# Mix stage of a decoder layer: the four gate units of the input projection moved to the end of the unit order

## The chip, the cores and the metric

The kernel runs on one core of one Trainium2 chip. A time is the device time of the whole program in microseconds (us). The engines are PE (TensorE, the matrix engine), DVE (VectorE), ACT (ScalarE), POOL (GpSimd) and SP (SyncE, which issues DMAs). Each runs its own list of instructions in a fixed order.

## The reference

One decoder layer over 512 prompt tokens and 8 sequences of 4 new tokens, in float32:

```python
x <- LN1(alpha*x + 0.5*SwiGLU_1(x))
x <- LN2(alpha*x + W_out[concat(attn_group(x), hgrn_group(x))])
x <- LN3(alpha*x + 0.5*SwiGLU_2(x))

z = x @ w_in
qa, ka, va, qh, fh, ih, gh = jnp.split(z, IN_SPLITS, axis=-1)
...
logf = jnp.log(lbh + (1.0 - lbh) * jax.nn.sigmoid(zf))
kh = (1.0 - lbh) * jax.nn.sigmoid(-zf)
qh = jax.nn.silu(qh)
```

The attention group has 8 heads of 64, with rotary positions and a dilated sliding window over keys, in the prompt and against cached keys and values for the new tokens. The other group has 4 HGRN2 heads: a gated recurrence S_t = diag(f_t) S_{t-1} + (1-f_t) outer i_t, with output o_t = S_t^T q_t, a root-mean-square norm per head, and a gate: the output is multiplied by silu(gh). The gate enters only there, at the very end of a head.

## The kernel before

The 544 columns (16 new tokens, 512 of the prompt, 16 new tokens) lie in two halves `a` of 272. Each float32 product is made of three matmuls, xH*wH, xL*wH and xH*wL, where H is the part rounded to the fast matmul format and L what is left (ACT makes H at L332, DVE makes L at L334). The mix stage, between the first FFN and the output projection, has 28 units of the input projection. A unit is 128 output columns: 2 halves x 8 blocks of the contraction x 3 = 48 matmuls (L315, L316, L317). The table `WIN` sets their order: an entry (c, i) is head group c (0 to 3) and kind i: 0 q, 1 k, 2 v, 3 forget gate f, 4 HGRN q, 5 HGRN value, 6 output gate. The weights lie in memory in this order and are fetched ahead through a ring of four. `rounds` runs the first four units side by side, and then one at a time.

What follows a unit hangs on its kind (`mixed`). After v, when q and k are there, comes `att_prompt(c)`: eight steps, four blocks of 128 queries (128, 256, 384 and 512 keys) times two heads. A step is: two score matmuls (L702) into a buffer `ps_a`; mask and negative maximum on DVE (L706, with a readout); exponential on ACT (L708); reciprocal and multiplication on DVE (L709, L710); one to four transpositions on PE (L679); a copy on ACT (L717). After each block of queries come the products with v (L726). Buffers `ps_a` and `aw` are two and three deep. `att_sample`, after head groups 1 and 3, handles the new tokens; it multiplies with cached values in tiles `kv`, fetched three deep by SP from `in_cv` (L784, L790).

After the HGRN value unit comes `hgrn(c)`, with two scans over the columns on DVE (L822, L825), and at its end a function `end`: mean of squares by matmuls (L954), a reciprocal root from logarithm and exponential (table load L435, L443, L446, L453 to L455), products with it, and `update`, which forms the new states (vm at L813, L973, L976). A gate unit makes tanh and a copy of its columns on ACT (L550, L551), their product on DVE (L552), and `gate` multiplies the head's output by it (L964). Two lines choose the order of the two: in `mixed`

```python
                        if WIN[j + 1] != (c, 6):
                            part["end"] = part["end"]()
```

runs `end` at once, without the gate, if the next unit is not the head's own gate, and leaves `gate` for later. Otherwise `end(gs)` runs with the gate unit, and applies the gate first and the norm after it. The order is fixed when the kernel is built: a scheduler simulates the engines over the program as it is written, and lays down a list for each engine. After the mix stage `project` splits the eight head outputs (L332, L334 to xH, xL) and multiplies by w_out; its first units are begun in the tail of the mix stage as their inputs come.

Of the kernel before, what the change touches and what calls it, by code (L numbers as in the profile page):

```python
# [64 lines left out]
def free(t, offset, dims):  # L65
# [3 lines left out]


WIN = (
    (0, 0), (0, 4), (0, 3), (0, 5), (0, 6), (0, 1), (1, 3), (0, 2), (1, 4), (1, 0), (1, 1), (1, 5), (1, 2), (2, 3),
    (2, 0), (2, 4), (2, 1), (2, 2), (1, 6), (2, 5), (2, 6), (3, 0), (3, 1), (3, 2), (3, 4), (3, 3), (3, 5), (3, 6),
)


# [1139 lines left out]
```

## Time and profile before

| | us |
|---|---|
| median of three runs | 1137.05 |
| lowest and highest | 1135.55, 1137.87 |
| profiled execution | 1141.93 |
| span of its instructions | 1140.1 |

The profiled execution had a mean granted clock of 0.982 of TensorE's full speed. A profile line that begins with two numbers and a bar at the end of its name (`| 6.2, 435 |`) gives busy time in us and the mean of one instruction in ns; a timeline row gives start and length in us, and in brackets what it waited for; a window row gives the stretch, its length, busy time and instructions of PE, weight loads, DVE, ACT and POOL, then the granted clock, the share of the DMA engines and GB/s.

### The profile page before, as it was taken

Reading aid. Unit: us, or ns where it says so; the run is one execution under the profiler, and the core shown is the slowest. Engines: PE = TensorE matmul, PEld = TensorE weight load, DVE = VectorE, ACT = ScalarE, POOL = GpSimd, SP = SyncE. Lnnn points to the kernel's source line nnn. Section 1 sums busy time; section 2 is a strip of 40 time slices with the busy share of each in tenths; the row PEclk is TensorE's granted clock in tenths of the full one; section 3 lists DMA queues with packets and bytes.
Section 4 is the critical chain, followed back from the end, with each engine's and each line's share of the span. In section 5 each row is a group of like instructions: output and inputs, shape, how many; then the busy total and the mean of one; then the engine's idle time right before and its main releaser. Section 6 shows DMA issues by size and latency. Waiting matters only on the chain.

```text
span 1140.1 us, 21927 instructions
## 1 busy us (share of the span) xinstructions
PE 1094.2 (96%) x8666; PEld 1047.1 (92%) x8666; DVE 780.7 (68%) x1282; ACT 570.6 (50%) x1123; POOL 373.8 (33%) x420
## 2 busy tenths in 40 slices
PE   7899999999999999999999988988999999999995
PEld 7899999999999988878997858978999999999995
DVE  6868857865776965664746646788687578567766
ACT  5435533552554675566456643465355235425544
POOL 2513412430343444231411301345143125214336
PEclk9899999999999999999999978999999999999998
DMA  7344444454415385376736624504533432332122
GB/s 247 104 130 154 154 144 148 126 194 149 128 44 195 112 276 168 122 261 228 238 105 223 240 98 161 184 17 171 171 130 102 136 111 89 89 103 92 41 72 79
DMA packets 46168, 163.49 MB, mean 143 GB/s; under 512 B 6512, under 2 KB 10224, under 8 KB 45040
## 3 DMA queue, kind: packets, MB, share of 16 engines
q1 hardware_dynamic: 46064, 162.08, 43.0%
q8 instruction: 68, 1.11, 0.4%
q14 instruction: 36, 0.29, 0.1%
HBM read 150.79 MB, written 42.60 MB: 170 GB/s over the span
## 4 chain that ended last, share of the span: by engine, by line
PE 82%; DVE 7%; DMA 4%; ACT 3%; issue 2%; POOL 2%; SPq 0%; POOLq 0%; DVEq 0%; ACTq 0%
PE ps_d L278 20%; PE ps_h L278 10%; PE ps_d L316 7%; PE ps_d L315 7%; PE ps_d L317 7%; PE ps_a L278 5%; PE ps_a L316 3%; PE ps_a L315 3%; PE ps_a L317 3%; PE ps_h L317 2%; PE ps_h L315 2%; PE ps_h L316 2%; DVE wL L334 2%; PE ps_s L754 1%; PE ps_a L679 1%
## 5 line engine op out<-in xcount | busy, mean ns | idle before, releaser
L334 DVE TENSOR_TENSOR wL<-ws,wH 128x1024 fp32r<-128x1024 f32 (+3 forms) x141 | 174.2, 1236 | 80.8 <-ACT wH L332 77.7
L332 ACT ACTIVATE wH<-ws 128x1024 fp32r<-128x1024 f32 (+3 forms) x141 | 129.3, 918 | 183.4 <-PE ps_d L278 49.3
L1008 POOL TENSOR_TENSOR h<-hx,h 128x272 fp32r<-128x272 f32 x88 | 98.6, 1122 | 159.7 <-ACT h L1007 153.4
L334 DVE TENSOR_TENSOR wL<-sw,wH 128x1024 fp32r<-128x1024 f32 x78 | 117.1, 1503 | 40.2 <-ACT wH L332 40.1
L315 PE MATMUL ps_d<-xH,wH 128*128 128x272 f32 x456 | 136.2, 299 | 4.7 <-ACT xH L332 4.3
L316 PE MATMUL ps_d<-xL,wH 128*128 128x272 f32 x456 | 137.4, 301 | 3.2 <-DVE xL L405 3.0
L317 PE MATMUL ps_d<-xH,wL 128*128 128x272 f32 x456 | 135.2, 297 | 0.5 <-DVE wL L334 0.5
L332 ACT ACTIVATE wH<-sw 128x1024 fp32r<-128x1024 f32 x78 | 82.6, 1059 | 81.8 <-PE ps_d L278 29.5
L225 POOL TENSOR_TENSOR sw<-ws,sw 128x512 f32<-128x512 f32 x38 | 55.3, 1456 | 157.3 <-DVE sw L222 137.5
L315 PEld LDWEIGHTS ps_d<-xH,wH 128*128 128x128 f32 x456 | 87.4, 192 | 9.2 <-ACT xH L332 5.0
L278 PE MATMUL ps_d<-xH,wL 128*128 128x272 f32 x320 | 92.9, 290 | 1.9 <-DVE wL L334 1.9
L316 PEld LDWEIGHTS ps_d<-xL,wH 128*128 128x128 f32 x456 | 87.6, 192 | 7.5 <-DVE xL L405 3.7
L278 PE MATMUL ps_d<-tH,wH 128*128 128x272 f32 x320 | 92.9, 290 | 0.0
L278 PE MATMUL ps_d<-tH,wL 128*128 128x272 f32 x320 | 92.9, 290 | 0.0
L278 PE MATMUL ps_d<-tL,wH 128*128 128x272 f32 x320 | 92.9, 290 | 0.0
L220 POOL TENSOR_TENSOR sw<-ws 128x512 f32<-128x512 f32 x38 | 53.2, 1401 | 120.7 <-issue 48.1
L278 PE MATMUL ps_d<-xL,wH 128*128 128x272 f32 x320 | 92.4, 289 | 0.0
L278 PE MATMUL ps_d<-xH,wH 128*128 128x272 f32 x320 | 92.2, 288 | 0.0
L317 PEld LDWEIGHTS ps_d<-xH,wL 128*128 128x128 f32 x456 | 87.6, 192 | 4.1 <-issue 2.7
L315 PE MATMUL ps_d<-h,wH 128*128 128x272 f32 x240 | 69.2, 288 | 0.0
L317 PE MATMUL ps_d<-h,wL 128*128 128x272 f32 x240 | 69.0, 288 | 0.0
L316 PE MATMUL ps_d<-h,wH 128*128 128x272 f32 x240 | 68.9, 287 | 0.0
(412 smaller groups left out, 3600.8 us busy)
## 6 DMA issues: line engine op xcount, KB each, us to landing
ws<-in_w2gu SPq DMA_DIRECT2D x42, 512.0 KB, 3.9
ws<-in_w1gu SPq DMA_DIRECT2D x41, 512.0 KB, 4.5
ws<-in_win SPq DMA_DIRECT2D x28, 512.0 KB, 4.2
out_ck_out<-in_ck SPq DMA_DIRECT2D x16, 640.0 KB, 5.7
out_cv_out<-in_cv SPq DMA_DIRECT2D x16, 640.0 KB, 5.5
kv<-in_ck SPq DMA_DIRECT2D x16, 640.0 KB, 6.3
kv<-in_cv SPq DMA_DIRECT2D x16, 640.0 KB, 5.0
ws<-in_w1d SPq DMA_DIRECT2D x24, 384.0 KB, 3.2
```

The costliest lines, as they stand in the source:

```text
L220: g.tensor_tensor(s2[:, lo], a21, a22, op=OP.add)
L225: g.tensor_tensor(s2[:, hi], a12, s1[:, hi], op=OP.subtract)
L278: nc.tensor.matmul(ps, w[:, k, :], y, start=first and i == 0, stop=last and i == 2, skip_group_check=True)
L315: mm(o, H[:, k, :], x[0], start=first, stop=False)
L316: mm(o, H[:, k, :], x[1], start=False, stop=False)
L317: mm(o, L[:, k, :], x[0], start=False, stop=last)
L332: a = self.nc.scalar.activation(H, x, AF.Copy)
L334: v = self.nc.vector.tensor_tensor(L, x, H.bitcast(F32), op=OP.subtract)
L679: self.nc.tensor.transpose(out, x, self.ident[:n, :n])
L754: last = mm(ps[w, :384], self.qsz[:, i, s, 32 * (b + x):32 * (b + x) + 32], kc[x][:, i, 2 * s:2 * s + 3].rearrange("p s d -> p (s d)"), st ...
L1008: nc.gpsimd.tensor_tensor(L, x, H.bitcast(F32), op=OP.subtract)
```

## The change

Only the table changes. Three gate units, (0,6), (1,6) and (2,6), move from places 5, 19 and 21 to the end, ahead of (3,6), which was last already. By the two lines above, heads 0, 2 and 3 now run `end` without their gate, as head 1 did, and all four multiply by the gate after the norm.

```diff
 WIN = (
-    (0, 0), (0, 4), (0, 3), (0, 5), (0, 6), (0, 1), (1, 3), (0, 2), (1, 4), (1, 0), (1, 1), (1, 5), (1, 2), (2, 3),
...
+    (2, 4), (2, 1), (2, 2), (2, 5), (3, 0), (3, 1), (3, 2), (3, 4), (3, 3), (3, 5), (0, 6), (1, 6), (2, 6), (3, 6),
 )
```

On PE, at the end of the stage: the sixth to eighth steps of the last attention. The names are those of the program, `aw` the probabilities, `ps_a` the scores or their transpositions, and 315 to 317 projection matmuls. Before, from the scores of the sixth step on:

```order
L702 MATMUL ps_a_7647<-klo_4814,qst_7416 128x384
L927 MATMUL ps_h_8165<-ivs_8142,ats_4818 32x256 x4
L930 MATMUL ps_h_8165<-st_8047,smp_8163 32x256 x4
L315 MATMUL ps_d_8349<-xH0_8291,wH_7861 128x272
...
L679 MATMUL ps_a_7655<-mats_69,aw_7650 128x128 x3
L702 MATMUL ps_a_7667<-kst_7498,qst_7416 128x512
L702 MATMUL ps_a_7667<-klo_4814,qst_7416 128x512
L954 MATMUL ps_h_8252<-E2_8051,mats_69 128x272
...
L679 MATMUL ps_a_7675<-mats_69,aw_7670 128x128 x4
```

In the new order, from the last matmul of the output projection's second block on:

```order
L317 MATMUL ps_d_8427<-xH0_8291,wL_8156 128x272
L679 MATMUL ps_a_7441<-mats_69,aw_7436 128x128 x3
L702 MATMUL ps_a_7447<-kst_7299,qst_7216 128x384
L702 MATMUL ps_a_7447<-klo_4814,qst_7216 128x384
L679 MATMUL ps_a_7455<-mats_69,aw_7450 128x128 x3
L702 MATMUL ps_a_7467<-kst_7299,qst_7216 128x512
L702 MATMUL ps_a_7467<-klo_4814,qst_7216 128x512
L973 MATMUL ps_h_8004<-vm_8005,ks3_7944 128x512
...
L679 MATMUL ps_a_7475<-mats_69,aw_7470 128x128 x4
L702 MATMUL ps_a_7482<-kst_7299,qst_7216 128x512
L702 MATMUL ps_a_7482<-klo_4814,qst_7216 128x512
L679 MATMUL ps_a_7490<-mats_69,aw_7485 128x128 x4
```

The norm's mean matmuls (L954) and the new tokens' state products (L927, L930), which stood among the last steps, have moved ahead of them, and a state product (L973) has come in.

On ACT, around the last head's norm. Before, the table load and logarithms stood between the copies and exponentials of the last steps:

```order
L717 ACTIVATE aw_7659<-ps_a_7655 128x384
L956 ACTIVATE ef_8062<-ps_h_8253 128x1
L435 ACT_TABLE_LOAD
L443 ACTIVATE E2_8051<-ps_h_8253,eps_71 128x272
L443 ACTIVATE E2_8051<-ps_h_8252,eps_71 128x272
L708 ACTIVATE aw_7670,stat_7577<-aw_7670,stat_7577 128x512
```

Now they stand ahead of the fifth step's exponential, `aw_7436`, with the last gate's work and five splits between:

```order
L435 ACT_TABLE_LOAD
L443 ACTIVATE E2_7852<-ps_h_7987,eps_71 128x272
L443 ACTIVATE E2_7852<-ps_h_7986,eps_71 128x272
L717 ACTIVATE aw_7401<-ps_a_7423 128x256
L332 ACTIVATE wH_8221<-ws_8220 128x1024
L550 ACT_TABLE_LOAD
L550 ACTIVATE gs_8252<-ps_d_8257 128x272
L551 ACTIVATE sw_8282<-ps_d_8257 128x272
L332 ACTIVATE xH1_8293<-z0_5612 128x272
...
L708 ACTIVATE aw_7436,stat_7377<-aw_7436,stat_7377 128x384
```

On DVE, around the seventh step of the last attention (`aw_7470`; before `aw_7670`). Before:

```order
L710 TENSOR_SCALAR aw_7650<-aw_7650,stat_7577 128x384
L964 SCALAR_TENSOR_TENSOR z1_8181<-z1_8181,gs_8217 128x544
L706 ISA aw_7670,stat_7577<-ps_a_7667,maskp_4808 128x512
L706 ISA stat_7577 128x1
L709 RECIPROCAL stat_7577<-stat_7577 128x1
```

Now:

```order
L710 TENSOR_SCALAR aw_7450<-aw_7450,stat_7377 128x384
L813 TENSOR_TENSOR z1_7982<-z1_7982,cum_7880 128x272
L813 TENSOR_TENSOR vm_8005<-vs3_7945,mats_69 96x512
L964 SCALAR_TENSOR_TENSOR z1_7982<-z1_7982,gs_8252 128x544
L706 ISA aw_7470,stat_7377<-ps_a_7467,maskp_4808 128x512
L706 ISA stat_7377 128x1
L334 TENSOR_TENSOR xL0_8292<-z1_7982,xH0_8291 128x272
L976 SCALAR_TENSOR_TENSOR st_7848<-st_7848,E1_7851,ps_h_8004 128x128 x4
L813 TENSOR_TENSOR vm_8013<-vs3_7945,mats_69 96x512
L334 TENSOR_TENSOR xL1_8294<-z1_7982,xH1_8293 128x272
L709 RECIPROCAL stat_7377<-stat_7377 128x1
```

The head's last norm product, the gate and parts of its state update now stand around this step's mask and division. After the mix stage the orders of the engines agree again.

More of the change, by code (lines that the diff above doesn't have):

```diff
@@ L71 @@
 WIN = (
-    (0, 0), (0, 4), (0, 3), (0, 5), (0, 6), (0, 1), (1, 3), (0, 2), (1, 4), (1, 0), (1, 1), (1, 5), (1, 2), (2, 3),
-    (2, 0), (2, 4), (2, 1), (2, 2), (1, 6), (2, 5), (2, 6), (3, 0), (3, 1), (3, 2), (3, 4), (3, 3), (3, 5), (3, 6),
+    (0, 0), (0, 4), (0, 3), (0, 5), (0, 1), (1, 3), (0, 2), (1, 4), (1, 0), (1, 1), (1, 5), (1, 2), (2, 3), (2, 0),
+    (2, 4), (2, 1), (2, 2), (2, 5), (3, 0), (3, 1), (3, 2), (3, 4), (3, 3), (3, 5), (0, 6), (1, 6), (2, 6), (3, 6),
 )
```

## The prediction, made before the changed kernel was run

> **What bounds the kernel now.** I read the page's shares and its slices first, then the table by windows over the slices in which PE dips, then PE's waits there, PE's timeline, and the chain.
>
> ```profile
> span 1140.1 us, 21927 instructions
> PE 1094.2 (96%) x8666; PEld 1047.1 (92%) x8666; DVE 780.7 (68%) x1282; ACT 570.6 (50%) x1123; POOL 373.8 (33%) x420
> PE   7899999999999999999999988988999999999995
> PEclk9899999999999999999999978999999999999998
> ```
>
> PE is the bound, and a slice is 28.5 us: PE and its granted clock dip together in the slices that begin at 656 and 684 us, the end of the mix stage. (PE's other dip in the middle, from 741 us, is LN2, behind this change.) Windows around that place, with instruction counts, and next to last the granted clock:
>
> ```profile
> 440.00:640.00 200.00, 198.78 (x1675) 172.79 (x1675) 118.18 (x269) 119.41 (x271) 48.58 (x92) 1.00 0.58 199
> 640.00:660.00 20.00, 19.39 (x202) 15.87 (x201) 13.85 (x40) 12.11 (x36) 8.37 (x22) 1.00 0.55 205
> 660.00:680.00 20.00, 17.61 (x113) 11.95 (x112) 7.08 (x24) 7.82 (x28) 0.00 (x0) 0.66 0.29 94
> 646.30:689.20 42.90, 33.82 (x266) 24.71 (x264) 21.92 (x67) 21.76 (x66) 2.06 (x8) 0.81 0.36 129
> ...
> PE ps_a L679 <- DVE aw L710: 6.9, 3, 3.1
> PE ps_s L784 <- DMA kv<-in_cv: 2.1, 2, 1.5
> ```
>
> From 440 to 640 us PE hardly pauses, so an order that keeps it fed there gains nothing. The last prompt attention runs from 646.3 (its first scores) to 689.2 (its last transpositions). In it PE issues 266 instructions; at the pace of 640 to 660 (202 in 20.00 us, 0.099 each) they need 26.3 us. So 42.9 - 26.3 = 16.6 us are lost there, the only loss that this change can reach. 9.0 of them are the two waits; the other 7.6 are mostly instructions at a clock of 0.66. Its anatomy on PE and on the chain (start, length, engine, what):
>
> ```profile
> 632.09 0.29 PE L316 MATMUL ps_d<-xL,wH 128*128 128x272 f32 x1
> ...
> 634.48 0.29 PE L317 MATMUL ps_d<-xH,wL 128*128 128x272 f32 x1
> 637.72 0.63 PE L679 MATMUL ps_a<-mats,aw 128*128 128x128 f32 x4 [0.24 <-DVE aw L710]
> 669.60 0.52 PE L702 MATMUL ps_a<-klo,qst 128*128 128x384 f32 x1
> 672.26 0.88 PE L679 MATMUL ps_a<-mats,aw 128*128 128x128 f32 x3 [0.73 <-DVE aw L710]
> 685.17 0.63 PE L679 MATMUL ps_a<-mats,aw 128*128 128x128 f32 x4 [3.14 <-DVE aw L710]
> 685.87 0.40 PE L702 MATMUL ps_a<-klo,qst 128*128 128x512 f32 x1
> 689.24 1.09 PE L679 MATMUL ps_a<-mats,aw 128*128 128x128 f32 x4 [2.98 <-DVE aw L710]
> ...
> 644.87 4.62 DMA kv<-in_cv
> 658.59 6.56 DMA kv<-in_cv
> 673.14 0.64 PE ps_a L702 x2
> 690.33 0.23 PE ps_a L315
> 693.05 0.23 PE ps_a L315
> ```
>
> A projection matmul starts every 0.126 us (20 between 632.09 and 634.48); a unit of 48 is 6.0. An attention step is scores (L702), DVE's mask and maximum (L706), ACT's exponential (L708), DVE's division (L709, L710), transpositions (L679): bare, 672.26 - (669.60 + 0.52) = 2.1 us for 384 keys and 689.24 - 686.27 = 3.0 for 512. PE loses what other work does not cover of that. The clock already drops after waits of 1.5 us, and at 690 a projection matmul takes 0.23.
>
> **The change, part by part.** No work is added or removed: the same 28 units, the same bytes, the same 8 attention steps a head group, the same instructions for every norm and gate. Two things move. First, gates 0, 1 and 2 move behind everything else: 18.1 us of matmuls that fed the middle. The middle keeps its cover by the order: between scores and transpositions stand at least 3.6 us of PE work in every earlier head group, against 3.0 bare. I cost it at nothing; if the cover fails, rival C gives the price. The first attention starts about 5 us earlier and the last one with 25.1 instead of 27.3 units issued, so 13.6 us more projection work lies behind its start. Counted in the two orders at the paces of the rows, that work covers its first five steps (5.6, 4.9, 5.9, 7.3 and 5.2 us each, before 3.3, 4.5, 5.7, 3.6 and 0.6), but its last three steps (0, 1.1 and 0) stay as bare as before. Also, each stored gate pass becomes a product of its own (L964) after the norm instead of before it, for heads 0, 2 and 3. Durations for these steps, ACT then DVE:
>
> ```profile
> L332 ACT ACTIVATE wH<-ws 128x1024 fp32r<-128x1024 f32 x5 | 5.3, 1055 | 3.4 <-PE ps_d L316 3.3
> L708 ACT ACTIVATE aw<-aw,stat 128x384 f32<-128x384 f32 x4 | 2.5, 613 | 2.2 <-DVE stat L706 2.2
> L435 ACT ACT_TABLE_LOAD x2 | 2.6, 1283 | 0.0
> L717 ACT ACTIVATE aw<-ps_a 128x256 f32<-128x256 f32 x3 | 1.2, 384 | 5.9 <-PE ps_a L679 5.9
> L551 ACT ACTIVATE sw<-ps_d 128x272 f32<-128x272 f32 x4 | 1.6, 390 | 0.0
> 682.74 0.87 ACT E L443 x2
> 696.45 0.75 ACT L332 ACTIVATE xH<-z 128x272 fp32r<-128x272 f32 x2
> ...
> L334 DVE TENSOR_TENSOR xL<-z,xH 128x272 fp32r<-128x272 f32 x16 | 6.2, 435 | 1.2 <-ACT xH L332 1.2
> L706 DVE CUSTOM_DVE_ANT_0 aw<-ps_a,maskp 128x512 f32<-128x512 f32 x4 | 2.7, 685 | 0.0
> L813 DVE TENSOR_TENSOR vm<-vs,mats 96x512 fp32r<-96x512 f32 x4 | 2.7, 680 | 0.0
> L709 DVE RECIPROCAL stat<-stat 128x1 f32<-128x1 f32 x13 | 2.1, 160 | 8.5 <-ACT aw L708 8.5
> L710 DVE TENSOR_SCALAR aw<-aw,stat 128x512 f32<-128x512 f32 x4 | 1.9, 486 | 0.1
> L964 DVE SCALAR_TENSOR_TENSOR z<-z,gs 128x544 f32<-128x544 f32 x2 | 1.5, 726 | 6.4 <-ACT z L945 6.4
> L822 DVE TENSOR_TENSOR_SCAN E<-mats,sf 128x544 f32<-128x544 f32 x1 | 1.3, 1292 | 0.0
> L829 DVE SCALAR_TENSOR_TENSOR E<-sn,lbw,E 128x544 f32<-128x544 f32 x1 | 0.7, 731 | 0.0
> L813 DVE TENSOR_TENSOR sf<-E,rec 128x512 f32<-128x512 f32 x1 | 0.7, 678 | 0.0
> 694.25 1.12 DVE L976 SCALAR_TENSOR_TENSOR st<-st,E,ps_h 128x128 f32<-128x128 f32 x4 [3.50 <-PE ps_h L973]
> ```
>
> Now the end of the new order, from head 3's mean matmuls (L954) on:
> - *Fifth step.* ACT's queue there: table load 1.28, two logarithms 0.87, an attention copy 0.38, a weight split 1.06, the table back 1.28, gate pass and copy 0.78, five xH at 0.37 a piece (0.75 for two), the exponential 0.8 with its sum, two halves of the norm's root 0.75, a last xH 0.4: 9.5 us. Then xL on DVE, 0.44, and hand-offs: PE has the last input of the out projection at 10.2, ends its block at 10.5, and has 7.0 us of own work until then. Lost 3.5.
> - *Sixth.* Transpositions and scores of 384 keys at the low clock 0.88 + 0.64 = 1.5, bare step 2.1, one norm operation of about 0.44 (as the xL) ahead of the division: 4.1, of which 0.8 is work at full clock. Lost 3.3.
> - *Seventh.* DVE is the queue: the norm's product 0.43, vm 0.68, gate 0.73, mask 0.69 with its readout 0.08, then ahead of the division xL 0.44, four L976 1.12, vm 0.68, xL 0.44, reciprocal 0.16, division 0.49: 5.9. PE has 2.25 of work. Lost 3.7.
> - *Eighth.* Transpositions and scores 686.27 - 685.17 = 1.1, bare step 3.0 (four L976 lie beside the scores). Lost 3.0.
>
> Together 13.5. Ahead of that, two terms. In head group 2, its seventh step's mask now stands behind head 3's scan (L822, 1.29), two 544-wide products (0.73 each, as L829), a 512-wide one (0.68) and six short ones: about 4.9 us of DVE, an estimate with 0.25 for each short one. Mask 0.77, then the longer of exponential and the DVE work ahead of the division (a weight's low part, a split of keys, a short product: 2.3, estimated from such rows), and the division 0.65 make 8.6, against 6.7 of PE work in the new order between the two transpositions: 1.9 lost, against 0.4 in the step at 637.72 before. And the value cache (kv<-in_cv): PE waited 2.1 for it before, inside the 16.6. By the new order 5.1, 6.7 and 5.2 us of PE work now lie between the pairs that are used one after the other; between 0 (each lands as at 644.87, 4.62) and 4 (each as at 658.59, 6.56, with hand-offs), I take 0.6, nearer to the first, since two of three gaps exceed the mean of the two rows (5.6) or miss it by half a microsecond.
>
> Sum: after 13.5 + 1.9 + 0.6 = 16.0 lost; before 16.6 + 0.4 = 17.0. The change is **-1.0 us**. The profiled execution took 1141.93 (span 1140.1), 4.9 above the median of 1137.05; it would be 1140.9, and the median 1136.0. What a measurement of this kernel can tell is about 0.2%, 2.3 us.
>
> **The rivals.**
> - *A, faster.* The new cover counts and the queues do not. If ACT and DVE reach the attention's operations in time (another engine pace of a few tenths reorders who waits), the fifth step loses 0, the others their bare 2.1, 3.0 - 1.1 = 1.9, and 3.0: 7.0, not 13.5. That is -7.5 (1129.5); with half the queue delay -4 (1132.8). For it: before, the first five steps lost mostly to lack of cover. Against: ACT's and DVE's orders are fixed, and the rows ahead of the fifth and seventh steps are in them. A second form: the clock stays up. At 672 to 690 in before a row costs nearly twice its full-clock time; steps at full clock save some 0.7 each in three steps and the restart (13 matmuls from 690.33 to 693.05 at 0.23, 0.10 each) 1.3, so -4.4 in all (1132.6). [...]
> - *B, slower.* The sample attention's value blocks come too late. Two of its three gaps of PE work (5.1, 5.2) are shorter than 6.56, and PE's queue behind them holds the head group's attention. At 6.56 each plus hand-off: 1.9 + 0.5 + 1.9 = 4.3 in place of 0.6, so +2.7 (1139.7). It decides from 6.0 us a transfer, where the waits reach 1.7 and eat the gain.
> - *C, slower.* The middle loses its cover: 3.6 us against 3.0 leaves 0.6 for queues on DVE and ACT; three steps that are late by 1.3 each are +4 less the 1.0, 1140.
> - *The change does not act:* the units move by the order, so only in the sense that both ends lose the same; that is my forecast.
>
> **How the numbers follow.** My forecast, within 2.3 of no change, has 0.43; A 0.35 (its two forms 0.27 and 0.08); B 0.12; C 0.07, and 0.03 for other losses. So faster 0.35, same 0.43, slower 0.22. The range reaches to half of A's queue and beyond, 1130, and to B and C at 1141; the likeliest case alone spans 1134.8 to 1139.
>
> **What would show it.** After: windows over the last attention with the same instructions, 16 us above their pace at full clock; waits of L679 on L710 again three, near 3 us; ACT's table loads 22 still; in the middle, 440 to 630, no wait of L679 above a few tenths but head group 2's; L784's waits below 1 in sum. The forecast is wrong if the fifth step has no gap (A), or L784 waits 4 (B), or PE pauses between 460 and 580 (C).

## The result and the profile after

The changed kernel took 1143.4 us (median of five runs, 1142.35 to 1147.24), the kernel before 1136.15 in the runs beside it: a ratio of 1.0062, with a 95% interval of 1.0044 to 1.0080. It is slower by 7 us, where 1136 was forecast with a range up to 1141. The profiled execution took 1142.51 us.

The page after, with the same lines as before (PE's slices, then the granted clock):

```profile
span 1140.7 us, 21941 instructions
PE   8899999999999998999999988988999999999995
PEclk9899999999999999999999998999999999999998
```

Read alone, this looks little worse than before: the span is 0.6 us longer, the clock's dip in the last attention is shorter (9 and 8 in the slices from 656 and 684 us, where it was 7 and 8), and the one new mark is PE's 8 in the slice that begins at 428 us. The reason is that the first profile of before was of an execution 5 us above its median. A second profile of the unchanged kernel (the first experiment) has a span of 1133.8, and against that one the change shows. The stretches of the mix stage in that second profile of before (stretch, length, busy time and instructions of PE, weight loads, DVE, ACT and POOL, clock, DMA share, GB/s):

```profile
396.00:440.00 44.00, 39.97 (x306) 36.99 (x306) 29.35 (x50) 27.70 (x54) 24.97 (x48) 1.00 0.68 231
440.00:640.00 200.00, 198.78 (x1676) 172.83 (x1675) 118.23 (x271) 119.46 (x272) 48.64 (x94) 1.00 0.57 199
660.00:680.00 20.00, 14.10 (x130) 9.81 (x129) 9.22 (x28) 11.59 (x36) 0.00 (x0) 1.00 0.26 85
645.70:683.80 38.10, 28.60 (x268) 21.58 (x268) 22.07 (x67) 21.50 (x66) 2.37 (x8) 0.97 0.41 146
```

And in the changed kernel:

```profile
396.00:440.00 44.00, 37.75 (x285) 36.05 (x284) 30.93 (x51) 28.83 (x56) 27.20 (x49) 0.96 0.66 235
440.00:640.00 200.00, 197.50 (x1682) 167.54 (x1683) 114.65 (x271) 114.53 (x266) 51.69 (x111) 1.00 0.59 204
660.00:680.00 20.00, 17.18 (x138) 15.12 (x137) 12.58 (x32) 15.21 (x39) 0.00 (x0) 1.00 0.37 125
644.00:691.40 47.40, 38.23 (x303) 32.82 (x301) 31.77 (x86) 28.44 (x78) 0.00 (x0) 0.94 0.33 112
```

The first rows differ most for their length: from 396 to 440 us PE is busy 2.2 us less and issues 21 instructions fewer, at a clock of 0.96. From 440 to 640 it is idle 1.3 us more. The rows from 660 to 680 matter for their clock, which is 1.00 in both. The last rows are the last attention, from its first scores to its last transpositions.

PE's waits in the mix stage (396 to 720 us) after the change, the largest:

```profile
PE ps_a L679 <- DVE aw L710: 7.5, 5, 2.9
PE ps_h L899 <- DVE kt L893: 3.1, 1, 3.1
PE ps_h L884 <- POOL k L856: 1.2, 1, 1.2
PE ps_h L899 <- DVE S L905: 1.2, 1, 1.2
PE ps_h L973 <- DVE vm L813: 1.1, 1, 1.1
```

The second row did not exist before. L899 are head 0's first state products; `kt` is a copy on DVE of transposed keys (L893). PE's rows there, first before and then after:

```profile
432.57 0.60 PE L679 MATMUL ps_h<-mats,sn 128*128 128x128 f32 x4
436.62 0.83 PE L754 MATMUL ps_s<-kv,qsz 128*32 128x384 f32 x2
438.66 0.49 PE L899 MATMUL ps_h<-ivt,kt 128*128 128x128 f32 x2
```

```profile
430.41 0.60 PE L679 MATMUL ps_h<-mats,sn 128*128 128x128 f32 x4
432.47 0.28 PE L317 MATMUL ps_d<-xH,wL 128*128 128x272 f32 x1
435.89 0.58 PE L899 MATMUL ps_h<-ivt,kt 128*128 128x128 f32 x2 [3.14 <-DVE kt L893]
```

DVE in the changed kernel at that place, up to the copy:

```profile
427.40 0.71 DVE L877 COPY_PREDICATED at<-mats,ps_h 128x512 f32<-128x512 uint32 x1
431.49 0.72 DVE L630 TENSOR_TENSOR raw<-raw,sw 128x544 f32<-128x544 f32 x1 [3.38 <-POOL raw L628]
432.13 1.87 DVE L629 TENSOR_TENSOR sw<-sw,tabs 128x544 f32<-128x544 f32 x1
433.92 1.23 DVE L334 TENSOR_TENSOR wL<-ws,wH 128x1024 fp32r<-128x1024 f32 x1
435.07 0.68 DVE L893 COPY kt<-ps_h 128x512 f32<-128x512 f32 x1
```

And DVE's copy before, with the rope product ahead of it:

```profile
432.40 0.73 DVE L630 TENSOR_TENSOR raw<-raw,sw 128x544 f32<-128x544 f32 x1 [3.02 <-POOL raw L628]
...
435.71 0.68 DVE L893 COPY kt<-ps_h 128x512 f32<-128x512 f32 x1
```

DVE makes the copy at nearly the same time in both (435.71 and 435.07), behind a rope product (L630) that waits 3 us for POOL in both. What changed is when PE asks for it: with gate 0's unit ahead there were projection matmuls left until 436, and PE came to L899 after the copy had ended (435.71 + 0.68); without it, PE reaches L899 at 432.75 and stands.

### The profile page after: what moved, and what is told of

Same layout as the page of the kernel before. It is cut to its first block, busy times and chain, and to the rows that moved or that the text cites. A ratio compares the mean times of both kernels' runs of the same rounds, so it can differ in the third digit from the quotient of the medians.

```text
span 1140.7 us, 21941 instructions
## 1 busy us (share of the span) xinstructions
PE 1092.6 (96%) x8666; PEld 1047.3 (92%) x8666; DVE 778.2 (68%) x1282; ACT 570.7 (50%) x1123; POOL 372.2 (33%) x420
## 4 chain that ended last, share of the span: by engine, by line
PE 83%; DVE 7%; ACT 4%; DMA 2%; issue 2%; POOL 1%; SPq 0%; POOLq 0%; DVEq 0%; ACTq 0%
PE ps_d L278 20%; PE ps_h L278 10%; PE ps_d L315 7%; PE ps_d L317 7%; PE ps_d L316 7%; PE ps_a L278 5%; PE ps_a L316 3%; PE ps_a L315 3%; PE ps_a L317 3%; PE ps_h L317 2%; PE ps_h L315 2%; PE ps_h L316 2%; DVE wL L334 1%; PE ps_s L754 1%; PE ps_a L679 1%
```

## The experiments

First the ratios to the kernel before in the runs beside each, and what the profiles show; each profile is one execution. "Fifth unit" is the fifth entry of the table by kind and head group (k 0 is head group 0's key unit). "Front wait" is PE's largest wait between 428 and 440 us other than that of L884, which is there in every profile (1.6 to 1.7 us where a gate is fifth, 1.2 to 1.3 where none is). The last two columns are estimates: the time of the last attention's first scores, and then the time from there to its output copy (L729), each with the PE work that the orders put into it (by the paces of the rows) taken off, as the difference to the second profile of before. They say where time went; the ratio says how much. They hang on the paces that are taken: with each row's mean in place of its usual pace they move by up to 1 us, and no more should be read from them. They are left empty where they were not worked out.

| kernel | fifth unit | median | ratio, interval | front wait | ahead of the last attention | in it |
|---|---|---|---|---|---|---|
| before, second profile | gate 0 | 1135.7 | 0.9990 [0.9980, 1.0001] | L754 0.4 | 0 | 0 |
| before, first profile | gate 0 | | | L754 0.4 | +0.3 | +4.9 |
| changed, two profiles | k 0 | 1143.6 | 1.0057 [1.0042, 1.0072] | L899 3.1 | +5.7, +7.1 | +1.4, +2.2 |
| only gate 0 late | k 0 | 1142.6 | 1.0043 [1.0029, 1.0058] | L899 3.1 | +4.0 | +1.6 |
| gates 1, 2 late | gate 0 | 1133.4 | 0.9969 [0.9958, 0.9980] | L754 0.5 | +0.2 | -2.5 |
| gate 1 first | gate 1 | 1133.6 | 0.9978 [0.9968, 0.9987] | L754 0.4 | | |
| gates 3, 1, 2 last | gate 0 | 1138.3 | 1.0014 [1.0001, 1.0026] | L754 0.4 | +1.0 | +0.9 |
| changed, f 1 later | k 0 | 1139.7 | 1.0024 [1.0010, 1.0037] | L899 3.1 | +6.1 | -1.5 |
| gates 1, 2 late, f 1 later | gate 0 | 1130.1 | 0.9948 [0.9927, 0.9969] | L754 0.4 | -2.6 | -2.3 |
| gates 1, 2 late, gate 0 after f 1 | k 0 | 1140.4 | 1.0035 [1.0022, 1.0047] | L899 3.1 | +5.6 | -0.7 |
| changed, v 0 fifth | v 0 | 1142.1 | 1.0050 [1.0033, 1.0068] | L754 2.3 | +3.1 | +1.7 |
| changed, kt on ACT | k 0 | 1145.8 | 1.0079 [1.0065, 1.0093] | kt 2.6 | | |
| before, kt on ACT | gate 0 | 1136.7 | 1.0012 [0.9991, 1.0034] | L754 0.2 | | |

**The kernel before again.** No edit.

> The kernel before, unchanged, for a second profile: the first one's execution (1141.9) was 5 us above its median. Theory S (the first profile was a slow execution): the wait of PE for the value cache (kv from in_cv, 2.1 us in the first profile) is absent or shorter, the clock in the last attention is above 0.66, the last attention loses less than 16.6 us, and the execution takes 1135 to 1138. Rival: the loss in the tail is the same 16 us and the profiling itself costs the 5 us; then the second profile is near 1142 again with the same waits.

The profiled execution took 1135.62. Theory S is right about the execution, the clock and the loss, and wrong about the wait for the value cache, which is still there. PE's two groups of waits in the tail were the same to 0.2 us:

```profile
PE ps_a L679 <- DVE aw L710: 7.0, 3, 3.1
PE ps_s L784 <- DMA kv<-in_cv: 1.9, 2, 1.3
```

What differed was the clock: 1.00 from 660 to 680 us, not 0.66. By the count of the prediction (0.099 us an instruction) the last attention lost 38.1 - 268 x 0.099 = 11.6 us, not 16.6.

**The changed kernel again.** No edit.

> The changed kernel, unchanged, for a second profile on the same chip as the others: 1142 to 1145, ratio 1.005 to 1.008. If the wait of 3.1 us of PE for DVE's copy kt (L893) near 432 us belongs to the order, it is there again, between 2.5 and 3.5 us.

The wait for kt was 3.1 again, and the time 1143.6. The wait belongs to the order.

**Only gate 0 late; only gates 1 and 2 late.**

```diff
-    (0, 0), (0, 4), (0, 3), (0, 5), (0, 6), (0, 1), ...
+    (0, 0), (0, 4), (0, 3), (0, 5), (0, 1), ... (3, 5), (0, 6), (3, 6),
```

> Only gate 0 moves to the end, ahead of gate 3; gates 1 and 2 stay. Theory F (the front): head 0's recurrence loses the gate unit that lay beside its chain on DVE and POOL; PE waits about 3 us for kt (L893) near 432 us, and this kernel is 3 to 7 us slower than before. Theory T (the tail: the gates' work on ACT and DVE queues among the last attention's steps): with only two gates there this kernel is within 2 us of before.

```diff
-    ... (2, 2), (1, 6), (2, 5), (2, 6), (3, 0), ... (3, 5), (3, 6),
+    ... (2, 2), (2, 5), (3, 0), ... (3, 5), (1, 6), (2, 6), (3, 6),
```

> Gate 0 stays in its place, gates 1 and 2 move to the end, ahead of gate 3. Theory F: no wait at 432 us beyond the 1.7 us of before, and the time is within 2 us of before or a little faster. Theory T: 4 to 7 us slower than before, as the change itself, with waits of L679 on L710 near 3 us in the last three steps and a tail that loses more than the unchanged kernel's.

Theory F holds and theory T falls. Gate 0 alone costs 5.8 us against the runs beside it (1142.6 and 1136.8); gates 1 and 2 alone gain 3.4. Together they are not the sum, +2.4, but +6.8; why is not shown. The windows of the two, first only gate 0, then gates 1 and 2:

```profile
396.00:440.00 44.00, 37.66 (x296) 35.96 (x294) 30.35 (x50) 28.57 (x55) 26.74 (x49) 1.00 0.67 234
```

```profile
396.00:440.00 44.00, 39.94 (x306) 36.96 (x305) 29.45 (x50) 27.70 (x54) 24.94 (x48) 1.00 0.69 232
640.00:720.00 80.00, 72.68 (x601) 65.22 (x601) 48.10 (x115) 37.95 (x99) 10.37 (x11) 0.98 0.49 165
```

**Gate 1 in gate 0's place.** Gates 0, 2 and 3 are last; the stored pass of gate 1 waits for its head.

```diff
+    (0, 0), (0, 4), (0, 3), (0, 5), (1, 6), (0, 1), ... (3, 5), (0, 6), (2, 6), (3, 6),
...
+                        if "gs" in part:
+                            o[4 + c] = part["end"](part["gs"])
+                        elif WIN[j + 1] != (c, 6):
...
+                    if a == 1 and i == 6 and "end" in part:
```

> Gate 1 takes gate 0's early place (its stored pass waits for head 1, and is multiplied in ahead of head 1's norm); gates 0, 2 and 3 are the last three units. Theory F (what the early gate unit gives is PE work beside head 0's chain, whichever gate it is): no wait for kt above 1 us at 432, and the time is that of gates 1 and 2 alone moved, 1132 to 1136. Rival G (gate 0's own lateness costs, by what it queues in the tail): 1139 or more, with the front of the kernel before.

The time was 1133.6, as theory F says, with 0.4 of front wait. It does not matter whose gate is early, or that gate 0's own pass is late: a gate unit in the fifth place is what counts. A gate starts no chain of its own; that this is the reason is likely, but the run does not show it.

**The copy kt of head 0 on ACT, in the changed kernel and in the kernel before.**

```diff
+        if h == 0:
+            A(kt.rearrange("p b d -> p (b d)"), ps, AF.Copy)
+        else:
+            v.tensor_copy(kt.rearrange("p b d -> p (b d)"), ps)
```

> The changed kernel with one copy of head 0 (kt, L893) on ACT in place of DVE, where it stood behind a split of weights and two rope products. Theory Q (the front's loss is that wait in DVE's queue, and what follows from it): the 3.1 us wait at 432 us falls below 1, and the time falls by 2 to 5 us, to 1139 to 1142. Rival N (not enough work on PE there, whatever the queue: the next step of head 0 waits instead, for POOL, ACT or the products with S): the wait only changes its name and the time stays within 1.5 us of the changed kernel's 1143.6.

> The control of the run above: the same edit on the kernel before, where PE does not wait for kt. Both theories: within 1.5 us of before (1136.8).

Theory Q falls as far as the edit could test it: the wait did not go. PE waits 2.6 for ACT's copy instead (the edit moves the lines, so L899 is L902 here), which stands behind work that follows the same rope. The wait changed its name, as rival N says, but the time, 1145.8, is 2.2 above the changed kernel's, outside N's range too. What removing the wait alone would be worth stays open. The control stays within 0.6 of the runs beside it.

```profile
PE ps_h L902 <- ACT kt L894: 2.6, 1, 2.6
```

**Gates 3, 1, 2 at the end.**

```diff
-    ... (3, 5), (1, 6), (2, 6), (3, 6),
+    ... (3, 5), (3, 6), (1, 6), (2, 6),
```

> Gate 0 early as before, and the last units are gates 3, 1, 2 in this order, so that head 3 multiplies by its gate before its norm, and the last head's norm starts a unit or two later, with gates 1 and 2 as cover for the sixth and seventh attention steps (7.1 and 4.9 us of PE work by the order, against 2.4 and 0.7 with gates 1, 2, 3). If the bare steps of the last attention set its end: 1130 to 1132.5, 1 to 3 us below gates 1, 2, 3. If the chain on ACT and DVE sets it whatever the cover: 1133 to 1136.

1138.3: 5 us above gates 1, 2, 3, so neither expectation. The cover was moved to the sixth and seventh steps, but new waits came: 3.2 for an input of the output projection (at 680 us), 1.9 in the attention and 1.7 ahead of it, at the new tokens' products (L927). The 1.7 of L884 is the front's, as before. From 640 to 720 us PE's waits come to 8.9 in sum, against 7.2 with gates 1, 2, 3; where the rest of the 5 us comes from is not shown.

```profile
PE ps_d L315 <- ACT xH L332: 3.2, 1, 3.2
PE ps_a L679 <- DVE aw L710: 1.9, 1, 1.9
PE ps_h L884 <- POOL k L856: 1.7, 1, 1.7
PE ps_h L927 <- ACT aw L708: 1.7, 1, 1.7
```

**Head 1's forget gate (f 1) one place later, in the changed kernel and with gates 1 and 2 late.**

```diff
-    ... (1, 3), (0, 2), (1, 4), ...
+    ... (0, 2), (1, 3), (1, 4), ...
```

> The changed kernel with one more exchange in the table: head 1's forget gate (1,3) and head 0's v (0,2) change places, so that two units, not one, stand between head 0's value unit and head 1's forget gate, as in the kernel before; all four gates stay last. Theory F1 (the early gate unit gave the distance between head 0's chain and the next forget gate, which uses the same single buffers): the wait for kt at 432 us falls below 1 and the time falls to 1131 to 1137. Rival F2 (what the early gate unit gave was a unit without work on POOL and the rope's queue on DVE; v and k in its place do not give that): a wait of 2 to 4 us stays in the front, and the time is 1140 to 1144.

> Gates 1 and 2 late, gate 0 early, with the same exchange of (1,3) and (0,2). The distance is there twice over, so F1 expects no further gain: within 2 us of gates 1 and 2 moved alone (1133.4). If an earlier start of the first attention (by 4 us of PE work in the order) moved the end of the stage, it would be 1129 to 1131.

In the changed kernel the wait at L899 stayed at 3.1, against F1 (the profile puts it down to a weight split on ACT that ends with the copy, both at 436.3), yet the time fell to 1139.7, just below F2's range: its gain lies, by the estimate, in the last attention (-1.5 in place of +1.4 to +2.2). With gates 1 and 2 late and gate 0 early the median is 1130.1, the lowest of this study, with a ratio of 0.9948. That is 3.3 below gates 1 and 2 late, or 2.4 by the ratios, whose intervals still meet. F1 did not expect a gain there; the other branch of the expectation, by which an earlier start of the first attention moves the end, had named 1129 to 1131, and that attention starts at 452.1 in place of 457.4. Beside L884's it has no front wait above 0.4, and PE is busy without a pause from 440 to 640 us:

```profile
396.00:440.00 44.00, 39.96 (x307) 36.98 (x306) 28.66 (x48) 26.78 (x53) 24.94 (x47) 1.00 0.72 247
440.00:540.00 100.00, 99.99 (x855) 86.99 (x857) 58.23 (x134) 64.04 (x146) 23.34 (x51) 1.00 0.55 192
540.00:640.00 100.00, 100.00 (x861) 85.99 (x854) 63.70 (x146) 58.00 (x134) 26.98 (x62) 1.00 0.59 208
```

**Gate 0 two places later, with gates 1 and 2 late.**

```diff
-    ... (0, 5), (0, 6), (0, 1), (1, 3), (0, 2), ... (1, 6), (2, 6), (3, 6),
+    ... (0, 5), (0, 1), (1, 3), (0, 6), (0, 2), ... (1, 6), (2, 6), (3, 6),
```

> Gates 1 and 2 late, and gate 0 two places later than before: after head 0's k and head 1's forget gate, ahead of head 0's v. F1 expects the loss of the front (the forget gate follows at the changed kernel's distance): 1136 to 1141. F2, or any theory by which a gate unit near head 0's chain is enough: 1132 to 1135.

The time was 1140.4, with the wait of 3.1 back: against "a gate near head 0's chain is enough". It differs from gates 1 and 2 late (1133.4) in nothing but gate 0's place, and this puts 7 us on that place. It agrees with F1's time, but the pair above had shown that F1's distance does not remove the wait.

**The v unit of head 0 fifth.** In `mixed` the attention starts when k and v are both there.

```diff
-    ... (0, 5), (0, 1), (1, 3), (0, 2), (1, 4), ...
+    ... (0, 5), (0, 2), (0, 1), (1, 3), (1, 4), ...
...
-                    if a == 1 and i == 2:
+                    if a == 1 and i and {"kraw", "vT"} <= set(part):
```

> The changed kernel with head 0's v unit (0,2) as the fifth unit, the place gate 0 had, ahead of the key unit (0,1); the attention of head group 0 then starts with the key. All four gates stay last, and the last two attentions have the same PE work between scores and transpositions as in the changed kernel. Theory P (the front's wait comes from a unit with rope work, POOL's and DVE's, in the fifth place; v has none): the wait for kt (L893) near 432 us falls from 3.1 to below 1, and the time to 1137 to 1141, with the rest of the loss in the last attention. Rival (only a unit without any successors there, a gate, keeps PE busy up to kt): the wait stays at 2.5 or more and the time is 1141 to 1145.

Between the two. The wait for kt went, as P expects, but a wait for POOL's copies of the queries came in its place, and the time, 1142.1, is the rival's:

```profile
PE ps_a L679 <- DVE aw L710: 7.2, 5, 2.9
PE ps_s L754 <- POOL qsz L662: 2.3, 1, 2.3
PE ps_h L899 <- DVE S L905: 1.7, 1, 1.7
```

So what is shown: the loss is set by the fifth place. All kernels without a gate there, seven profiles of six kernels, have a front wait of 2.3 to 3.1; all with one, seven profiles of six kernels, have 0.5 or less. With L884's wait added it is 3.6 to 4.5 against 1.8 to 2.2. Not shown is why the middle, from the first attention's scores (454 us in the changed kernel) to the last one's, costs about another 3 us by the estimate in every kernel without an early gate for which it was worked out, the one with v fifth among them. The visible waits there make up less than half: of 0.5 us and more, 2.0 us in sum after the change (0.8 at 506 us for ACT, 1.2 at 571 for DVE) and 1.0 before.

## Why the prediction was wrong

- *The middle keeps its cover, costed at nothing: the step that failed.* I counted PE work only between attention scores and transpositions, which begin at some 455 us, and there the cover held: L679 waits 0.4 us in sum from 440 to 640, 0.2 before. Gate 0's unit covered another chain, head 0's recurrence through POOL's rope and DVE's queue, 20 us earlier. My windows began at 440, so I called the last attention the only loss that the change can reach, though the same profile has PE idle for 4 us from 396 to 440 (busy 39.95 of 44.00). Signs of that chain stood there: PE waits 1.7 for POOL at L884 (429.6 us) and 0.4 at L754 (437.9), and between the two it has projection matmuls to do while DVE comes to the copy. Ahead of the last attention the change loses 5.7 to 7.1 us by the estimate, about half of it in the front and half in the middle; of the second half the cause stays open. Rival C named a middle without cover, with +4, but put it in the attentions and gave it 0.07.
- *The loss in the last attention before, 16.6: mis-sized.* It was that of one execution 5 us over its median; the second profile has 11.6 with the same waits. I had the sign of it in hand, 1141.93 against a median of 1137.05, and took the 4.9 us off at the end as a constant, though they lay in the very term that I let the change act on.
- *The last attention after, 13.5 + 0.6: right in sum, in part by luck.* It took 47.4 us with 303 instructions; with the 38.1 - 11.6 = 26.5 us of work of before and an estimated 7.4 more by the orders it lost 13.5, good to about 1 us. The parts do not agree as well. Step by step: fifth 3.5 forecast, waits of 1.0 and 1.2; sixth 3.3, a wait of 2.9; seventh 3.7, waits of 1.1 and 0.5; eighth 3.0, a wait of 2.5. The waits sum to 9.2; most of the rest is likely the lower clock (0.74 from 680 to 700), of which the forecast had only a part. The rows of PE that carry the sixth to eighth step:

```profile
682.25 0.87 PE L679 MATMUL ps_a<-mats,aw 128*128 128x128 f32 x3 [2.86 <-DVE aw L710]
686.75 0.50 PE L973 MATMUL ps_h<-vm,ks 96*128 96x512 f32 x1 [1.11 <-DVE vm L813]
687.79 0.63 PE L679 MATMUL ps_a<-mats,aw 128*128 128x128 f32 x4 [0.54 <-DVE aw L710]
691.38 1.09 PE L679 MATMUL ps_a<-mats,aw 128*128 128x128 f32 x4 [2.45 <-DVE aw L710]
```

- *13.6 us more work behind the last attention's start: mis-sized.* That counted projection units. Recurrence and sample work moved ahead of the start meanwhile; by all PE work in the orders it is an estimated 7.4.
- *Head group 2's seventh step, 1.9, and the value cache, 0.6.* Measured: its seventh step waits for nothing that the profile shows (transpositions at 630.3 us), its sixth 0.4, and the value cache is not waited for. Rival B did not happen.
- *Rival A* did not happen either: the fifth step had its gap. Nor did its second form, a clock that stays up: it was 1.00 from 660 to 680 us, but 0.74 and 0.66 from 680 to 700 in the two executions.

With 11.6 in place of 16.6 and the last attention as forecast, the sum would have been some +4 us for the change, 1141; the front and the middle, costed at nothing, are the rest. The two errors weigh about the same: 5.0 us from the baseline, and, against the 1.5 that I had put ahead of the last attention, 4.2 to 5.6 from the front and the middle.

## What to carry to other kernels

When a unit is taken out of an order, ask of each chain around its old place, not only of the stage's main chain, what PE does while DVE, POOL or ACT make the next operand; the new order shows how much earlier PE arrives, the trace of before shows when the operand is ready. A profile of an execution that lies off the median is not a baseline for a term: find out which stage holds the difference before sizing anything there. A table of such an order can be searched in parts: two of its three moves were a gain of 0.3%, and the third turned them into a loss.

## What the runs showed of the hardware

The same order did not give the same clock. The kernel before, with the two groups of waits in the last attention equal to 0.2 us, held 1.00 from 660 to 680 us in one execution and 0.66 in another, and the last attention took 38.1 and 42.9 us. Nor did the same wait: with the front's wait of 3.1 us the clock from 396 to 440 us was 0.96 and 0.95 in two executions of the changed kernel and 1.00 with only gate 0 late. Nor did the low clock stand beside a long wait: in the first profile it was 0.66 from 660 to 680 us with no wait above 1.54 us there, and no wait in that whole attention was above 3.14. What makes the clock fall in one execution and not in another is not shown.
